# Earlier fetches of two sets, y stored in long rows, and gate loads in two halves, in the last stages of a gated decoder layer

## The chip, the cores and the metric

The kernel runs on one core of a Trainium2 chip. The metric is the device time of one execution in microseconds (us). The core's engines work side by side: TensorE (PE in the profile; PEld is its weight load) multiplies, VectorE (DVE), ScalarE (ACT) and GpSimd (POOL) work on elements, and SyncE (SP) issues transfers between DRAM and the core's memory. Each engine takes its instructions in order, so an instruction that waits holds up those behind it on the same engine.

## The reference

One decoder layer on 2048 rows of width 1024, in float32. From u = x * (1 + scale) + shift one wide product gives queries, keys, values, an attention gate, a pool input, a pool gate and two merge gates m_a and m_p. Then:

```
A = (sliding window attention * silu(attn_gate)) @ W_attn_proj
P = (causal pool, mixed and scaled, * silu(pool_gate)) @ W_pool_proj
y = (sigmoid(m_a) * A + sigmoid(m_p) * P) @ W_out * (1 + gate)
out = LayerNorm(alpha * x + y)
```

The last three lines and the two merge gates are what the change is about: the products with W_attn_proj, W_pool_proj and W_out behind the second attention.

## The kernel before, in words

The rows are worked on in two halves of 1024 (s = 0, 1). Each float32 product is made from split operands: a high part rounded to float32r and a low remainder, multiplied in three matmuls. A product of a 256 x 1024 piece of weights with a 1024 x 1024 operand goes by a scheme of seven block products in place of eight (B11, T1, T2, B21, T3, B22, T4), where the T's are sums and differences of blocks. The moving operand's seven blocks, each split, are the seven **sets** in SBUF; their raw blocks lie in DRAM in stores (`ain_d`, `pin_d`, `wo_d`), written by the attention and by `sums_to`. A pair of weight tiles is a **quad** (`Quad`, line 244 and on): `load` fetches it with three DMAs, `sum1`, `mid` and `late` make its sums on GpSimd, and `pair_split` (line 299 in the profile for the ScalarE part, 131 for the VectorE part) splits it for TensorE.

Behind the second attention the kernel runs six phases, in the loop at the end of the kernel function. Phase 0 finishes the last gate products. Phases 1 and 2 are the attention and pool projections for s = 0, phases 3 and 4 the same for s = 1; each has two groups of two quads. Phase 5 is the product with W_out, four groups of two quads; here y plays the part of the weights, and the rows y_d holds are loaded as quads (`out_quad`).

Within a phase `ring` goes through the groups. `back` does what a group has left after its fronts: for each quad T2 and B21, then T3 and B22, then T4, ten products of 12 matmuls. Then `front` does B11 and T1 for each quad of the next group, four products. After every product comes a `tick`; a group with a following one has ticks 0 to 13, 10 to 13 in the fronts. At a tick hooks run that are written for that place (a key (-1, p) is tick p of the phase's last group), and after them what `defer` has put off by that many ticks. So the order on SP is written out by hand, in program order (`sp` keeps each instruction behind the one traced before it on SP), while those written as `nc.scalar`, `nc.vector`, `nc.gpsimd` and `nc.sync` may be moved by the planner that orders each engine's list; a quad's weight loads are among these.

The next phase's sets replace the current ones during its last group. `FETCH_AT` says at which tick each set's raw halves (512 KB each) are fetched, `SPLIT_AT` at which tick ScalarE and VectorE split them: B11's halves at ticks 2 and 3, T1's at 4 and 5. The fetch writes the memory that TensorE reads as the set's low part, so it waits for the last product with the old set.

A quad of phases 1 to 4 has four finished blocks of 128 x 512 and multiplies each with a block of a merge gate, 256 KB, loaded by `ahead` into one of eight buffers. `back` begins with all eight loads of its two quads. In phases 1 and 3, and in the first group of 2 and 4, ScalarE takes the sigmoid of each loaded block. In the pool phases VectorE multiplies (line 601), GpSimd adds to the attention's part (line 603), and the sum is y, which is stored three ticks later. Beside all this `sums_to` makes the T blocks of coming stores: loads (`spare<-ain_B` and the like), subtractions on GpSimd, stores (`ain_T<-spare` and the like).

Of the kernel before, what the change touches and what calls it, by code (L numbers as in the profile page):

```python
# [19 lines left out]
P = 128  # L20
D = 1024
S = 2048
# [37 lines left out]
def kernel(  # L60
# [58 lines left out]
    ain_d = [set_store(f"ain{s}") for s in range(2)]  # L119
    pin_d = [set_store(f"pin{s}") for s in range(2)]  # L120
    gates_d = {n: dp.tile([2, KT, 2, P, CH], F32, name=f"{n}_d") for n in ("ag", "pg", "ma", "mp")}
    y_d = dp.tile([S // P, P, KT, P], F32, name="y_d")

    def cols(t, n):
        return t[:, n * CH : (n + 1) * CH]
# [118 lines left out]
    class Quad:  # L244
# [7 lines left out]
        def load(self, ph, own, q=nc.sync, e=nc.gpsimd):  # L252
            self.w, self.a22 = ph.weights(), ph.last(own)
            x = self.w
            q.dma_start(x[:, 2, :], self.srcs[1][:, 0:CH])
            q.dma_start(self.a22, self.srcs[1][:, CH:])
            q.dma_start(x[:, 0::3, :], by_two(self.srcs[0]))
            if e is not None:
                self.sum1(e)
# [75 lines left out]

    def back(ph, grp, opened, nxt, own, tick):
        st = []
        for turn in range(2):
            for q in grp:
                if q.ahead:  # L340
                    q.ahead(ph, turn)
        for q, (a, b, c, w, *copy) in zip(grp, opened):
            p5 = ph.p("p5")
            if w is None:
                c = bank("lg")
                nc.scalar.copy(c, a)
                nc.scalar.copy(p5, b)
                w = pair_split(ph, q.second())[::-1]
                q.late()
                product(c, w[1], "T2")  # L350
            else:
                u2 = copy[0] if copy else ph.p("u2")
                if not copy:
                    nc.scalar.copy(u2, a)
                if c is None:
                    c = bank("lg")
                    product(c, w[1], "T2", True)
                nc.vector.tensor_tensor(c, c, u2, ALU.add)
                nc.scalar.copy(p5, b)
            tick()  # L360
            nc.vector.tensor_tensor(b, c, p5, ALU.add)
            if not copy:
                product(a, w[0], "B21")
            tick()
            q.consume(ph, 0, 0, a)
            st.append((q, b, c, p5))
        w = {}

        def ask(q):

            defer(1, lambda: q.load(ph, own, nc.sync, None))
            defer(3, lambda: q.sum1(nc.gpsimd))

        def third(x):
            w[x] = pair_split(ph, st[x][0].third())[::-1]
            if x < len(nxt):
                ask(nxt[x])

        def with_t3(x):
            q, b, c, p5 = st[x]  # L380
            product(c, w[x][1], "T3")
            tick()
            nc.vector.tensor_tensor(p5, c, p5, ALU.add)
            q.consume(ph, 1, 1, p5)

        def with_b22(x):
            q, b, c, p5 = st[x]
            product(b, w[x][0], "B22")
            tick()
            q.consume(ph, 0, 1, b)  # L390

        for x in range(len(st)):
            third(x)
            with_t3(x)
            with_b22(x)
        for q in nxt[len(st) :]:
            ask(q)
        for q, b, c, p5 in st:
            w = half_split(ph, q.a22)
            product(c, w, "T4")  # L400
            tick()
            q.consume(ph, 1, 0, c)
# [29 lines left out]
    def defer(ticks, f):  # L432
        due.append((now[0] + ticks, len(due), f))
# [48 lines left out]

    SPLIT_AT = (2, 3, 4, 5, 6, 7, 11, 12, 13, 14, 15, 16, 17, 18)

    FETCH_AT = {"B11": 0, "T1": 0, "T2": 3, "B21": 4, "T3": 7, "B22": 8, "T4": 10}

    def set_steps(ph, store):

# [16 lines left out]
            todo.append((at, lambda n=name, h=half: split(n, h)))  # L505
        return sorted(todo, key=lambda t: t[0])

    def planned(hooks, ph, store, last, pending={}):
        if last:
            pending["steps"] = set_steps(ph, store)  # L510
        for p, f in pending["steps"]:
            if (p < 14) == last:
                hooks.setdefault((-1, p) if last else (0, p - 14), []).append(f)
        return hooks


# [79 lines left out]
    def pool_quad(s, m):  # L596
        gates, ahead = gates_ahead("mp", s, m, m < 4)

        def consume(ph, mi, t, src):
            g = gates.pop((mi, t))  # L600
            nc.vector.tensor_tensor(g, src, g, ALU.mult)
            dst = ta[m + mi][:, t * CH : (t + 1) * CH]
            nc.gpsimd.tensor_tensor(dst, g, dst, ALU.add)  # L603
            k = 8 * s + 4 * t
            to = y_d[k : k + 4, :, m + mi, :].rearrange("s p q -> p s q")
            defer(3, lambda: sp.dma_start(to, dst.rearrange("p (s q) -> p s q", s=4)))

        return Quad((wpp[m], wpp[m + 1]), consume, ahead)

# [41 lines left out]
    def last_norm(row, z):  # L651
# [6 lines left out]
        for n, q in enumerate((nc.sync, nc.scalar)):  # L658
            zn = cols(z, n)
            nc.vector.scalar_tensor_tensor(zn, zn, rs, cols(vec["lnb"], n), ALU.mult, ALU.add)  # L660
            q.dma_start(out[row * P : (row + 1) * P, n * CH : (n + 1) * CH], zn)

    def out_quad(k):
        def consume(ph, mi, n, src):
            row = k + mi
# [9 lines left out]
                else:  # L675
                    norm_row(ph, row, z)

        return Quad(tuple(y_d[k + i].rearrange("p k q -> p (k q)") for i in range(2)), consume)

# [773 lines left out]
    with Pools("mix", spare=4, p=2, c=8) as ph:  # L1455
# [15 lines left out]
        for i, (groups, store) in enumerate(phases):  # L1471
# [2 lines left out]
                planned(hooks, ph, store, False)  # L1474
            after, nxt = None, []
            if i + 1 < len(phases):
                planned(hooks, ph, phases[i + 1][1], True)
                nxt = phases[i + 1][0][0]
                after = lambda tick, nxt=nxt: [front(ph, q, tick) for q in nxt]
            else:  # L1480
# [67 lines left out]
```

## Time and profile before

| | |
|---|---|
| median of 3 runs | 1733.91 us (1731.9 to 1734.55) |
| profiled execution | 1734.67 us, span 1732.9 us |
| TensorE busy in the span | 1665.9 us (96%) |
| VectorE, ScalarE, GpSimd busy | 1257.8, 964.5, 1063.0 us |
| DMA engines, 1375 to 1455 us | 0.86 busy, 307 GB/s |
| phases 1 to 4 | about 1240 to 1577 us |

A row of the timeline gives the start in us, the time to the end of the row's instructions, engine, line, operation, what is written from what, sizes, how many instructions, and in brackets the idle time ahead of it and what ended it. L56 is the line of the helper that records most operations, so rows are told apart by their tiles: `w_set` is a split weight, `set_B` and `set_T` the B and T sets, `g` a gate block, `wide` the attention part and y, `W` and `A` a quad's raw weights. `lg` and `mm` are banks of TensorE's result memory: T2, T3 and T4 go to `lg`, the others to `mm`. A row that begins with SPq is SP's queue: the time of one is that of issuing it, with its wait for the ones in the row but not for the first.

### The profile page before, as it was taken

The page shows a single profiled execution, that of the slowest core. Times are in us where ns is not written, and L with a number is a line of the kernel's source. Part 1 is how long each engine was busy: PE and PEld are TensorE (multiplying, and loading weights), DVE is VectorE, ACT ScalarE, POOL GpSimd, SP SyncE. Part 2 cuts the span into 40 slices and gives each one's busy share as a digit, 9 for nine tenths or more (in the row PEclk, how much of TensorE's full clock was granted, in tenths as well). Part 3 has the DMA queues.
Part 4 walks back from the last instruction along what each step waited for, and adds up shares of the span by engine and source line. Part 5 has one row for each costly group of instructions (what it writes and reads, how often), then busy time and mean ns, then how long its engine had stood idle before and what let it go on. Part 6 is the DMA issues. An engine that isn't in the chain of part 4 may idle for free.

```text
span 1732.9 us, 24692 instructions
## 1 busy us (share of the span) xinstructions
PE 1665.9 (96%) x8056; PEld 1392.2 (80%) x8056; DVE 1257.8 (73%) x2256; ACT 964.5 (56%) x2002; POOL 1063.0 (61%) x782
## 2 busy tenths in 40 slices
PE   6899999999999999999999999999999899999997
PEld 5688888888888788887888888888777678777885
DVE  5966565787778768458578777786769487859777
ACT  4544446677677654334567676765644345434552
POOL 2054427686867837862476778594656796657442
PEclk9999999999999999999999999999999899999999
DMA  9378853323433377866533334235887788786432
GB/s 352 126 287 286 222 184 110 116 100 122 153 109 98 130 260 270 286 214 206 187 110 104 131 118 152 86 117 188 313 311 260 276 299 298 268 289 234 158 142 102
DMA packets 188721, 336.79 MB, mean 194 GB/s; under 512 B 18208, under 2 KB 43952, under 8 KB 188592
## 3 DMA queue, kind: packets, MB, share of 16 engines
q1 hardware_dynamic: 185472, 330.96, 55.4%
q10 hardware_dynamic: 3088, 4.23, 1.0%
q8 instruction: 64, 1.05, 0.3%
q14 instruction: 65, 0.53, 0.1%
q0 software_dynamic: 32, 0.02, 0.0%
HBM read 227.96 MB, written 110.33 MB: 195 GB/s over the span
## 4 chain that ended last, share of the span: by engine, by line
PE 44%; POOL 7%; DVE 6%; DMA 5%; issue 4%; ACT 2%; SPq 1%; POOLq 0%; DVEq 0%; ACTq 0%
PE mm L56 28%; PE lg L56 12%; PE pv L56 2%; POOL wide L603 2%; PE pt L56 2%; DVE w_set L131 2%; POOL spare L56 1%; POOL W L262 1%; SPq L56 1%; DVE set_T L56 1%; ACT w_set L299 1%; DMA W<-in_wap_dram 1%; DMA g<-ma_d 1%; POOL W L266 1%; POOL w_set L56 1%
## 5 line engine op out<-in xcount | busy, mean ns | idle before, releaser
L56 PE MATMUL mm<-set_B,w_set 128*128 128x512 f32 x2664 | 660.1, 395 | 9.9 <-ACT w_set L299 5.2
L56 PEld LDWEIGHTS mm<-set_B,w_set 128*128 128x128 f32 x2664 | 499.1, 190 | 119.1 <-DVE w_set L131 8.4
L56 PE MATMUL mm<-set_T,w_set 128*128 128x512 f32 x1824 | 457.5, 397 | 4.5 <-POOL w_set L56 1.2
L56 PE MATMUL lg<-set_T,w_set 128*128 128x512 f32 x1728 | 424.7, 396 | 20.3 <-DVE w_set L131 8.6
L56 PEld LDWEIGHTS lg<-set_T,w_set 128*128 128x128 f32 x1728 | 326.9, 191 | 96.6 <-DVE w_set L131 14.6
L56 PEld LDWEIGHTS mm<-set_T,w_set 128*128 128x128 f32 x1824 | 337.2, 189 | 77.0 <-DVE mm L56 4.4
L131 DVE TENSOR_TENSOR w_set<-W,w_set 128x1024 fp32r<-128x1024 f32 x138 | 207.9, 1507 | 173.9 <-ACT w_set L299 164.0
L299 ACT CAST w_set<-W 128x1024 fp32r<-128x1024 f32 x138 | 144.9, 1050 | 283.1 <-PE mm L56 165.6
L56 POOL TENSOR_TENSOR w_set<-W,w_set 128x512 fp32r<-128x512 f32 x132 | 171.9, 1310 | 101.2 <-ACT w_set L56 91.3
L262 POOL TENSOR_TENSOR W<-W,A 128x512 f32<-128x512 f32 x46 | 71.5, 1554 | 218.1 <-DMA A<-in_win_dram 75.5
L56 ACT ACTIVATE L<-L,nm 128x257 f32<-128x257 f32 (+1 forms) x256 | 127.1, 498 | 26.4 <-DVE nm L56 20.3
L56 POOL TENSOR_TENSOR W<-W 128x512 f32<-128x512 f32 x82 | 108.3, 1334 | 51.6 <-DVE sm L56 30.3
L271 POOL TENSOR_TENSOR W<-W 128x512 f32<-128x512 f32 x46 | 74.7, 1624 | 98.5 <-DVE w_set L131 89.0
L56 POOL TENSOR_TENSOR spare<-spare 128x512 f32<-128x512 f32 x68 | 121.0, 1782 | 13.0 <-DMA spare<-ain_B 9.1
L56 DVE CUSTOM_DVE_ANT_0 L<-lg,bt,nsink 128x256 f32<-128x256 f32 (+1 forms) x256 | 111.6, 473 | 20.4 <-DMA bt<-e_rep 9.4
L56 ACT CAST w_set<-W 128x512 fp32r<-128x512 f32 (+1 forms) x164 | 100.1, 626 | 38.2 <-POOL W L56 25.7
L56 DVE COPY o<-pv 64x256 f32<-64x256 f32 x128 | 54.3, 424 | 81.1 <-PE pv L56 79.8
L56 ACT CAST pth<-pt 128x512 fp32r<-128x512 f32 (+1 forms) x128 | 72.8, 568 | 63.3 <-PE pt L56 62.9
L56 ACT ACTIVATE L<-L,sm 128x256 f32<-128x256 f32 (+1 forms) x128 | 64.3, 503 | 68.1 <-DVE sm L56 67.8
L266 POOL TENSOR_TENSOR W<-W 128x512 f32<-128x512 f32 x44 | 75.0, 1705 | 34.2 <-DVE w_set L131 25.1
L267 POOL TENSOR_TENSOR W<-W 128x512 f32<-128x512 f32 x44 | 74.4, 1691 | 31.6 <-DMA W<-in_win_dram 26.0
L56 DVE TENSOR_SCALAR L<-L,sm 128x256 f32<-128x256 f32 (+1 forms) x128 | 89.9, 702 | 0.0
(225 smaller groups left out, 2468.3 us busy)
## 6 DMA issues: line engine op xcount, KB each, us to landing
W<-in_win_dram SPq DMA_DIRECT2D x42, 512.0 KB, 5.5
W<-in_win_dram SPq DMA_DIRECT2D x42, 256.0 KB, 3.7
A<-in_win_dram SPq DMA_DIRECT2D x42, 256.0 KB, 4.6
ag_d<-sig SPq DMA_DIRECT2D x32, 256.0 KB, 5.1
pg_d<-sig SPq DMA_DIRECT2D x32, 256.0 KB, 4.6
pg<-pg_d SPq DMA_DIRECT2D x32, 256.0 KB, 3.1
pin_B<-fin SPq DMA_DIRECT2D x32, 256.0 KB, 2.1
ag<-ag_d SPq DMA_DIRECT2D x32, 256.0 KB, 2.8
```

Source lines behind the costliest of these rows:

```text
L56: return lambda *args, **kw: self.tc.keep_in_program_order(op(*args, **kw))
L131: engine.tensor_tensor(dst, src, as32(hi), ALU.subtract)
L262: e.tensor_tensor(self.w[:, 1, :], self.w[:, 2, :], self.a22, ALU.add)
L266: e.tensor_tensor(x[:, 1, :], x[:, 1, :], x[:, 0, :], ALU.subtract)
L267: e.tensor_tensor(x[:, 2, :], x[:, 0, :], x[:, 2, :], ALU.subtract)
L271: e.tensor_tensor(x[:, 3, :], x[:, 3, :], x[:, 1, :], ALU.subtract)
L299: a.copy(by_two(hi), raw)
L603: nc.gpsimd.tensor_tensor(dst, g, dst, ALU.add)
```

## The change

Three things, all in the phases behind the second attention.

- The fetches of B11 and T1 for the next phase move from tick 0 of a phase's last group to ticks 12 and 13 of the group ahead of it. Where a phase has one group (phase 0), they stay at tick 0 of the last group.
- `back` begins with the four first gate loads of its two quads, and puts the other four off by two ticks.
- y lies in DRAM by blocks, as the gates do, so a block of 128 x 512 is stored in rows of 2 KB and not in four pieces of 512 bytes. A quad of phase 5 is then read in pieces of 512 bytes, with four DMAs of 256 KB in place of three.

```
-    y_d = dp.tile([S // P, P, KT, P], F32, name="y_d")
+    y_d = dp.tile([2, KT, 2, P, CH], F32, name="y_d")
...
         def load(self, ph, own, q=nc.sync, e=nc.gpsimd):
             self.w, self.a22 = ph.weights(), ph.last(own)
             x = self.w
+            if len(self.srcs[0].shape) == 3:
+                for dst, src, half in ((x[:, 2, :], 1, 0), (self.a22, 1, 1), (x[:, 0, :], 0, 0), (x[:, 3, :], 0, 1)):
+                    q.dma_start(dst.rearrange("p (k q) -> p k q", k=4), self.srcs[src][:, 4 * half : 4 * half + 4, :])
+                if e is not None:
+                    self.sum1(e)
+                return
...
     def back(ph, grp, opened, nxt, own, tick):
         st = []
-        for turn in range(2):
-            for q in grp:
-                if q.ahead:
-                    q.ahead(ph, turn)
+        for q in grp:
+            if q.ahead:
+                q.ahead(ph, 0)
+                defer(2, lambda q=q: q.ahead(ph, 1))
...
-    FETCH_AT = {"B11": 0, "T1": 0, "T2": 3, "B21": 4, "T3": 7, "B22": 8, "T4": 10}
+    FETCH_AT = {"B11": -2, "T1": -1, "T2": 3, "B21": 4, "T3": 7, "B22": 8, "T4": 10}
...
-    def planned(hooks, ph, store, last, pending={}):
+    def planned(hooks, ph, store, last, pending={}, groups=()):
         if last:
             pending["steps"] = set_steps(ph, store)
         for p, f in pending["steps"]:
             if (p < 14) == last:
-                hooks.setdefault((-1, p) if last else (0, p - 14), []).append(f)
+                at = (-1, p) if last else (0, p - 14)
+                if p < 0:
+                    at = (-2, 14 + p) if len(groups) > 1 else (-1, 0)
+                hooks.setdefault(at, []).append(f)
         return hooks
...
             nc.gpsimd.tensor_tensor(dst, g, dst, ALU.add)
-            k = 8 * s + 4 * t
-            to = y_d[k : k + 4, :, m + mi, :].rearrange("s p q -> p s q")
-            defer(3, lambda: sp.dma_start(to, dst.rearrange("p (s q) -> p s q", s=4)))
+            defer(3, lambda: sp.dma_start(y_d[s, m + mi, t], dst))
...
+    def y_row(row):
+        return y_d[row // 8, :, row // 4 % 2, :, row % 4 * P : (row % 4 + 1) * P].rearrange("k p q -> p k q")
...
-        return Quad(tuple(y_d[k + i].rearrange("p k q -> p (k q)") for i in range(2)), consume)
+        return Quad(tuple(y_row(k + i) for i in range(2)), consume)
...
-                planned(hooks, ph, phases[i + 1][1], True)
+                planned(hooks, ph, phases[i + 1][1], True, groups=groups)
```

## The prediction

> **What bounds the kernel.** I read the page first, then TensorE's rows in order of time behind the second attention (from about 1226 us), the waits, the DMA queue's rows of SP, and windows of 4 us.
>
> ```profile
> PE 1665.9 (96%) x8056; PEld 1392.2 (80%) x8056; DVE 1257.8 (73%) x2256; ACT 964.5 (56%) x2002; POOL 1063.0 (61%) x782
> ```
>
> TensorE is the bound, so the change can only win back what TensorE loses. In these stages every product is 12 matmuls, and the rows below stand 2.72 us apart where nothing waits. A group of two quads is 14 products: 38.08 us. These rows are the first product of each group (T2 of its first quad), from phase 1 to phase 5:
>
> ```profile
> 1277.99 2.88 PE L56 MATMUL lg<-set_T,w_set 128*128 128x512 f32 x12
> 1321.49 3.09 PE L56 MATMUL lg<-set_T,w_set 128*128 128x512 f32 x12
> 1359.78 2.98 PE L56 MATMUL lg<-set_T,w_set 128*128 128x512 f32 x12
> 1416.59 2.88 PE L56 MATMUL lg<-set_T,w_set 128*128 128x512 f32 x12
> 1454.78 2.88 PE L56 MATMUL lg<-set_T,w_set 128*128 128x512 f32 x12
> 1494.16 3.02 PE L56 MATMUL lg<-set_T,w_set 128*128 128x512 f32 x12
> 1532.38 2.88 PE L56 MATMUL lg<-set_T,w_set 128*128 128x512 f32 x12
> 1576.97 0.61 PE L56 MATMUL lg<-set_T,w_set 128*128 128x512 f32 x2
> ```
>
> The second groups of phases 1 to 4, which I call places 1 to 4, take 43.50, 56.81, 39.38 and 44.59 us: they lose 5.42, 18.73, 1.30 and 6.51 us, 31.96 in all. The first groups between them lose 0.1 to 0.2 each. So this is the most that the change can find here, and places 2 and 4 hold most of it. What ends the loss at these two, on TensorE and on ScalarE:
>
> ```profile
> 1378.50 1.22 PE L56 MATMUL lg<-set_T,w_set 128*128 128x512 f32 x2 [5.68 <-ACT w_set L299]
> 1388.50 2.89 PE L56 MATMUL lg<-set_T,w_set 128*128 128x512 f32 x12
> 1408.06 5.90 PE L56 MATMUL mm<-set_B,w_set 128*128 128x512 f32 x12 [3.08 <-ACT w_set L299]
> ```
>
> ```profile
> 1375.11 1.04 ACT L56 CAST set_B<-set_B 128x1024 fp32r<-128x1024 f32 x1 [8.39 <-DMA set_B<-ain_B]
> 1541.43 1.05 ACT L56 CAST set_B<-set_B 128x1024 fp32r<-128x1024 f32 x1 [7.49 <-DMA set_B<-wo_B]
> ```
>
> ScalarE, in order, stands 8.39 us at the split of the next phase's B11 because its data has not landed; the weight split that TensorE's T3 needs is queued behind it, and TensorE stands 5.68 us. The two matmuls behind it take 1.22 us, where the two at 1576.97 take 0.61. Place 4 has the same wait, 7.49 us.
>
> Why the data is late, on SP:
>
> ```profile
> 1271.54 5.78 SPq L56 DMA_DIRECT2D g<-ma_d  x8
> 1277.63 1.21 SPq L56 DMA_DIRECT2D set_B<-pin_B  x2
> 1359.07 5.22 SPq L56 DMA_DIRECT2D y_d<-wide  x2
> 1364.35 3.84 SPq L56 DMA_DIRECT2D g<-mp_d  x8
> 1368.76 1.23 SPq L56 DMA_DIRECT2D set_B<-ain_B  x2
> 1448.15 3.76 SPq L56 DMA_DIRECT2D g<-ma_d  x8
> 1452.00 1.28 SPq L56 DMA_DIRECT2D set_B<-pin_B  x2
> 1529.70 3.87 SPq L56 DMA_DIRECT2D g<-mp_d  x8
> 1533.66 1.44 SPq L56 DMA_DIRECT2D set_B<-wo_B  x2
> ```
>
> ```profile
> 1360.00:1364.00 4.00, 4.00 (x19) 3.16 (x18) 0.13 (x1) 0.00 (x0) 3.92 (x4) 1.00 0.21 64
> 1372.00:1376.00 4.00, 0.82 (x4) 0.36 (x2) 0.00 (x0) 0.89 (x1) 0.00 (x0) 1.00 1.05 407
> 1392.00:1396.00 4.00, 4.00 (x20) 3.30 (x19) 3.96 (x4) 0.71 (x1) 4.00 (x3) 1.00 1.06 405
> ```
>
> In each place eight gate loads go out ahead of the B11 fetch, and at place 2 SP first stood behind two y stores. The windows (busy PE, PEld, DVE, ACT, POOL, then clock, DMA share, GB/s) show the DMA engines at 0.21 just before and full from 1372 on: the fetch is asked for at the start of a jam.
>
> **The change, part by part.**
>
> *B11 and T1 asked for earlier.* They move from tick 0 of the last group to ticks 12 and 13 of the group ahead, past the eight gate loads. Each gets a wait in exchange: the set is being read by TensorE until the last B11 (T1) front ends. That is the start of the next product (first rows below; the second rows are issues from 1200 us on: how many, KB each, median us from issue to landing):
>
> ```profile
> 1275.27 2.88 PE L56 MATMUL mm<-set_T,w_set 128*128 128x512 f32 x12
> 1357.06 2.88 PE L56 MATMUL mm<-set_T,w_set 128*128 128x512 f32 x12
> 1452.06 2.88 PE L56 MATMUL mm<-set_T,w_set 128*128 128x512 f32 x12
> 1529.66 2.88 PE L56 MATMUL mm<-set_T,w_set 128*128 128x512 f32 x12
> ```
>
> ```profile
> set_B<-ain_B SPq DMA_DIRECT2D x10, 512.0 KB, 8.1
> g<-ma_d SPq DMA_DIRECT2D x32, 256.0 KB, 5.3
> y_d<-wide SPq DMA_DIRECT2D x32, 256.0 KB, 3.2
> A<-y_d SPq DMA_DIRECT2D x8, 256.0 KB, 3.4
> ```
>
> Place 2: B11's set is free at 1357.06, but SP reaches the fetch behind the first of the two y stores of 1359.07 (the second, of the last T4, comes after tick 12's hooks): 1359.5, 9.2 us earlier, into idle DMA. Even with the median 8.1 us it lands at 1367.6; ScalarE gets there at 1366.7 (1375.11 less 8.39). I take the whole 8.39 as gone and the following work on VectorE and POOL as that much earlier: gain 8.4. Not the 10.4 that T3 to T3 loses beyond the earlier stall (1388.50 less six products from 1359.78 is 12.4, of which some 2 precede it): POOL is busy 4.00 of 4 us from 1388 on, and the second stall, at 1408.06, waits for it. That stall is what is late next, and I keep it. Ends: 4.4 (the fetch behind both y stores, 1364.4) and 16.8 (all 18.73 but the first 2).
>
> Place 4: the set is free at 1529.66, SP issues at about 1529.8 instead of 1533.66: 3.9 us of the 7.49 go. Ends 0 and 6.5.
>
> Place 1: 1275.4 instead of 1277.63, and its T3 stalls come from a crowded ScalarE and VectorE, not from the fetch. I take 1 us of 5.42; ends -7.8 (below) and 5.4.
>
> Place 3: the set is free at 1452.06 and the fetch goes out at 1452.00 today: nothing to gain; 0, ends -7.9 and 1.3.
>
> In phase 0, with one group, the fetch stays where it is: 0.
>
> *Behind the new waits.* SP stands until TensorE is done; behind it are the last y store, stores of the sums, and the gate loads. T1's fetch goes out at the start of the group, its two issues take some 1.3 us, and then come the gates: 1279.3 instead of 1271.54 at place 1, 1365.7 instead of 1364.35, 1456.1 instead of 1448.15, 1533.7 instead of 1529.70: 7.8, 1.3, 7.9 and 4.0 later. Who waits: in the attention phases ScalarE's sigmoid, and VectorE's multiplication of the first finished bank. Place 3 shows the room:
>
> ```profile
> 1460.74 0.68 DVE L592 TENSOR_TENSOR wide<-mm,g 128x512 f32<-128x512 f32 x1
> 1461.34 1.72 DVE L131 TENSOR_TENSOR w_set<-W,w_set 128x1024 fp32r<-128x1024 f32 x1
> ```
>
> A gate asked for at 1456.1 lands by 1461.4 (5.3), and with 0.6 for the sigmoid the multiplication starts at 1462.0, 1.3 late; the weight split behind it ends at 1463.1 and T3 needs it at 1465.7 (1454.78 and four products). 2.6 us of room cover 1.3: I cost this at 0. Without that cover it is up to 7.9.
>
> That SP itself stands for TensorE is in its own waits (total us, times, longest):
>
> ```profile
> SPq L56 <- PE lg L56: 23.4, 14, 5.6
> ```
>
> The Trainium skill, "DMA: Bandwidth & Descriptors", section "Anatomy of one DMA", has the rule that speaks against this change: a semaphore wait stands at the issuing sequencer and not in the DMA engines, so whatever is queued behind the fetch is held with it; the row agrees. If nothing made room for that, the time would be the third rival's.
>
> *Gates in two halves.* Same sixteen loads a phase, four of them two ticks later, past tick 0's and tick 1's stores of sums. The late half serves B22 and T4, three products (8.2 us) or more behind its issue against a landing of 5.3: 0; end -3, where those stores wait long for POOL and the sigmoids of a first group stand ahead of T3's split.
>
> *y in rows of 2 KB.* 32 stores become long rows; the loads of the out stage become 512-byte rows, four issues a quad instead of three. A store with 512-byte rows lands after 3.2 us, a load with 2 KB rows after 3.4: the row length does not show. Eight more issues of about 0.4 us on SP lie beside products; a quad's load in the out stage has this much room:
>
> ```profile
> 1590.76 1.29 POOL L262 TENSOR_TENSOR W<-W,A 128x512 f32<-128x512 f32 x1 [5.56 <-DMA W<-y_d]
> 1605.38 2.88 PE L56 MATMUL mm<-set_B,w_set 128*128 128x512 f32 x12
> ```
>
> The sum is ready at 1592 and its front begins at 1605: a load twice as slow is still hidden. 0; ends -1.6 and 1.6, the 0.2 us between the two landings on each of eight quads.
>
> **Sum.** 8.4 + 3.9 + 1 + 0 = 13.3 us. The profiled execution took 1734.67 us (span 1732.9 and 1.8 around it), which gives 1721.4; the median of the three runs is 0.8 below it, so 1721 against 1733.91.
>
> **Rivals.**
>
> *Everything behind goes too.* If POOL, which now idles while VectorE stands, uses that time and the second stall at place 2 goes, and the tail of place 4: 16.8 + 6.5 + 5.4 = 28.7, or 1705. For it: POOL has no work in 1372 to 1376. Against: 4.00 of 4 later.
>
> *The fetch is not much earlier.* If at places 2 and 4 it gets out only behind the last y store: 4.4 and 2.5 (1531.1, when that store is out) instead of 8.4 and 3.9, less 1 for the sums: 6 us, 1728. For it: y stores hold SP 5.22 us here. Against: only one of them stands ahead of tick 12's hooks.
>
> *Slower: the gates are held.* The new wait on SP delays them by 7.8 + 1.3 + 7.9 + 4.0 = 21.0 us. If ScalarE's sigmoids or VectorE's multiplications stand ahead of the weight split of T2 or T3, this reaches TensorE. It decides from 13.3 of the 21.0 on; with 17 it is +3.7, 1738. For it: at place 1 ScalarE already stands for a gate, 3.47 us (row below). Against: the room at place 3; and this order of ScalarE is not fixed by the source.
>
> ```profile
> 1277.59 1.31 ACT L581 ACTIVATE g<-g 128x512 f32<-128x512 f32 x2 [3.47 <-DMA g<-ma_d]
> ```
>
> **How the numbers follow.** Forecast 0.55 (1714 to 1730), everything 0.14, not much earlier 0.12, gates held 0.19. A measurement of this kernel tells about 0.2% (3.5 us) from no change. Faster than that: 0.53 + 0.14 + 0.07 = 0.74; same: 0.02 + 0.05 + 0.02 = 0.09; slower 0.17. The range leaves out the lower half of the second case (0.07) and the upper half of the last (0.10): 1707 to 1736.
>
> **What would show it.** SP's rows should have the B11 fetch ahead of the gates at all four places, at place 2 by about 9 us; ScalarE's wait for set_B from ain_B should be gone and the one for wo_B about half; place 2 should take some 48 us, place 4 some 41, places 1 and 3 as before; in the out stage no product should wait for a load of y. Wrong would be: ScalarE or VectorE standing for g at places 1 or 3 with TensorE behind, or place 2's second stall grown by what the first gave up.

## The result and the profile after

The changed kernel takes 1728.22 us, the median of 12 runs (1726.14 to 1732.47), against 1734.23 for the kernel before on the same chip: a ratio of 0.9967, with a 95% interval from 0.9959 to 0.9975. That is 6.0 us faster, where 12.9 were forecast. The sign was right and the time lies inside the range, but the gain is under half of the forecast.

The profiled execution took 1731.03 us (span 1729.2), 3.6 us less than the one of before and 2.8 more than its own median. The two traces can therefore account for some 3.6 us; the rest of the 6.0 is known from the medians only. From the page of the changed kernel, the busy times:

```profile
PE 1664.1 (96%) x8056; PEld 1392.5 (81%) x8056; DVE 1254.5 (73%) x2256; ACT 964.2 (56%) x2002; POOL 1058.1 (61%) x782
```

The first product of each group on TensorE, as in the prediction (start, length, engine, line, operation, tiles):

```profile
1277.18 2.88 PE L56 MATMUL lg<-set_T,w_set 128*128 128x512 f32 x12
1317.18 3.07 PE L56 MATMUL lg<-set_T,w_set 128*128 128x512 f32 x12
1355.75 0.61 PE L56 MATMUL lg<-set_T,w_set 128*128 128x512 f32 x2
1410.07 2.88 PE L56 MATMUL lg<-set_T,w_set 128*128 128x512 f32 x12
1450.02 2.88 PE L56 MATMUL lg<-set_T,w_set 128*128 128x512 f32 x12
1492.36 2.88 PE L56 MATMUL lg<-set_T,w_set 128*128 128x512 f32 x12
1530.44 2.88 PE L56 MATMUL lg<-set_T,w_set 128*128 128x512 f32 x12
1572.79 0.61 PE L56 MATMUL lg<-set_T,w_set 128*128 128x512 f32 x2
```

Differences of neighbouring rows give the groups. Places 1 to 4 now take 40.00, 54.32, 42.34 and 42.35 us, where they took 43.50, 56.81, 39.38 and 44.59. So place 1 won 3.5, place 2 won 2.5, place 4 won 2.2, and place 3 lost 3.0. The first group of phase 3, which lost 0.1 before, takes 39.95 instead of 38.19: 1.8 lost. From the start of place 1 to phase 5 this is 295.61 us against 298.98, 3.4 less.

SP's rows show the fetches where they were expected. A row has start, time, queue, line, kind, tiles and how many issues it holds:

```profile
1273.07 1.89 SPq L56 DMA_DIRECT2D set_B<-pin_B  x2
1277.71 2.40 SPq L56 DMA_DIRECT2D g<-ma_d  x4
1356.89 1.19 SPq L56 DMA_DIRECT2D set_B<-ain_B  x2
1362.05 2.20 SPq L56 DMA_DIRECT2D g<-mp_d  x4
1445.90 1.89 SPq L56 DMA_DIRECT2D set_B<-pin_B  x2
1450.56 2.51 SPq L56 DMA_DIRECT2D g<-ma_d  x4
1526.33 1.89 SPq L56 DMA_DIRECT2D set_B<-wo_B  x2
1530.97 7.44 SPq L56 DMA_DIRECT2D g<-mp_d  x8
```

Counted from its group's start, the fetch goes out at +1.14 at place 2, where it was +8.98: 7.8 us earlier. At place 4 it is -4.11 instead of +1.28. The price is in the rows of g: at place 4 the gates, which went out at -2.68, now go out at +0.53, and their eight issues take 7.44 us.

What became of place 2, on TensorE, ScalarE and GpSimd of the changed kernel (in brackets the idle time ahead of a row and what ended it; L305 and L268 are the lines that the prediction's rows have as L299 and L262):

```profile
1370.85 2.56 PE L56 MATMUL lg<-set_T,w_set 128*128 128x512 f32 x10 [1.13 <-DVE w_set L131]
1392.66 5.34 PE L56 MATMUL mm<-set_B,w_set 128*128 128x512 f32 x12 [5.39 <-ACT w_set L305]
1403.34 4.07 PE L56 MATMUL mm<-set_B,w_set 128*128 128x512 f32 x10 [0.53 <-DVE w_set L131]
```

```profile
1363.04 1.99 ACT L56 CAST set_B<-set_B 128x1024 fp32r<-128x1024 f32 x2
1391.56 1.04 ACT L305 CAST w_set<-W 128x1024 fp32r<-128x1024 f32 x1 [9.52 <-DMA pin_T<-spare]
```

```profile
1389.06 1.25 POOL L612 TENSOR_TENSOR wide<-g,wide 128x512 f32<-128x512 f32 x1
1390.27 1.25 POOL L268 TENSOR_TENSOR W<-W,A 128x512 f32<-128x512 f32 x1
```

The same sum and the same front in the kernel before:

```profile
1393.53 1.73 POOL L262 TENSOR_TENSOR W<-W,A 128x512 f32<-128x512 f32 x1
1399.38 2.88 PE L56 MATMUL mm<-set_B,w_set 128*128 128x512 f32 x12
```

ScalarE splits B11 at 1363.04 without a wait: the 8.39 us are gone, and with them the stall of 5.68 at T3 (1.13 is left). But at the first front of phase 3, where TensorE did not wait before, it now stands for 5.39 us, and the twelve matmuls behind it take 5.34 where 2.88 is usual. The stall that the prediction kept, 3.08 us at the second front with twelve matmuls in 5.90 behind it, shrank to 1.37 and 0.53 us.

At the first front TensorE waits for ScalarE's split of a weight. That split starts 0.04 us behind the end of GpSimd's sum (line 268, `sum1`; 1390.27 and 1.25), so I take it to wait for the sum, although its row names a store. The sum stands in GpSimd's list behind additions into y (line 612). Counted from the group's start, TensorE is ready for this front at +31.5 us instead of +39.6, 8.1 earlier and so nearly the 8.4 forecast. The sum starts at +34.5 instead of +33.8: it did not come earlier at all. What the first stall gave up, the new one took.

### The profile page after: what moved, and what is told of

Read it like the earlier page. It is cut to its first block, busy times and chain, and to the rows that moved or that the text cites. A ratio compares the mean times of both kernels' runs of the same rounds, so it can differ in the third digit from the quotient of the medians.

```text
span 1729.2 us, 24722 instructions
## 1 busy us (share of the span) xinstructions
PE 1664.1 (96%) x8056; PEld 1392.5 (81%) x8056; DVE 1254.5 (73%) x2256; ACT 964.2 (56%) x2002; POOL 1058.1 (61%) x782
## 4 chain that ended last, share of the span: by engine, by line
PE 47%; POOL 7%; DVE 5%; DMA 4%; issue 4%; ACT 1%; SPq 0%; POOLq 0%; DVEq 0%; ACTq 0%
PE mm L56 30%; PE lg L56 13%; PE pv L56 2%; PE pt L56 2%; DVE w_set L131 1%; POOL spare L56 1%; POOL nxt L56 1%; POOL W L268 1%; POOL w_set L56 1%; POOL fin L56 1%; DMA W<-in_wpp_dram 1%; DMA W<-in_wap_dram 1%; DMA pin_T<-spare 1%; POOL wide L612 1%; DVE set_T L56 1%
## 5 line engine op out<-in xcount | busy, mean ns | idle before, releaser
L56 PE MATMUL lg<-set_T,w_set 128*128 128x512 f32 x1728 | 417.9, 392 | 10.0 <-DVE w_set L131 4.8
L131 DVE TENSOR_TENSOR w_set<-W,w_set 128x1024 fp32r<-128x1024 f32 x138 | 198.4, 1439 | 185.9 <-ACT w_set L305 172.8
L305 ACT CAST w_set<-W 128x1024 fp32r<-128x1024 f32 x138 | 144.8, 1050 | 291.0 <-PE mm L56 164.4
L268 POOL TENSOR_TENSOR W<-W,A 128x512 f32<-128x512 f32 x46 | 70.6, 1535 | 223.8 <-DVE set_T L56 58.2
L56 POOL TENSOR_TENSOR spare<-spare 128x512 f32<-128x512 f32 x68 | 117.2, 1725 | 12.6 <-DMA spare<-ain_B 8.7
```

What stands on the lines that cost most here:

```text
L56: return lambda *args, **kw: self.tc.keep_in_program_order(op(*args, **kw))
L131: engine.tensor_tensor(dst, src, as32(hi), ALU.subtract)
L268: e.tensor_tensor(self.w[:, 1, :], self.w[:, 2, :], self.a22, ALU.add)
L305: a.copy(by_two(hi), raw)
```

## The experiments

All kernels are timed against the kernel before. The times of the places come from each kernel's own profiled execution, by the same rows; y alone, which is no difference in time, moves place 1 by 2.0 us and place 3 by 3.3, so a difference of that size at one place counts only where rows show what made it. The last column is place 2 with the first group of phase 3, for a reason that comes out below. The last three kernels have the pinned sums too.

| kernel | ratio (95%) | place 1 | place 2 | place 3 | place 4 | place 2 + next group |
|---|---|---|---|---|---|---|
| before | 1 | 43.50 | 56.81 | 39.38 | 44.59 | 95.00 |
| changed | 0.9967 (0.9959 to 0.9975) | 40.00 | 54.32 | 42.34 | 42.35 | 94.27 |
| fetch alone | 0.9972 (0.9961 to 0.9982) | 42.89 | 50.97 | 39.95 | 42.25 | 91.02 |
| y alone | 1.0007 (0.9997 to 1.0016) | 41.47 | 56.32 | 42.69 | 42.97 | 94.51 |
| halves alone | 0.9957 (0.9943 to 0.9971) | 40.53 | 56.30 | 39.41 | 39.72 | 94.38 |
| changed, sums pinned | 0.9977 (0.9966 to 0.9988) | 40.67 | 49.99 | 41.97 | 42.51 | 90.00 |
| halves and fetch | 0.9964 (0.9952 to 0.9977) | 42.21 | 51.47 | 40.30 | 41.45 | 91.54 |
| changed, T1 late | 0.9968 (0.9957 to 0.9980) | 40.48 | 53.47 | 40.32 | 40.82 | 93.38 |
| halves, fetch at place 2 | 0.9949 (0.9934 to 0.9964) | 40.57 | 53.21 | 39.45 | 39.69 | 93.12 |
| the same, sums pinned | 0.9947 (0.9930 to 0.9963) | 40.38 | 50.89 | 39.43 | 39.65 | 91.08 |
| halves by one tick | 1.0034 (1.0022 to 1.0046) | 40.13 | 54.35 | 38.44 | 38.62 | 102.48 |
| pinned, B21 late | 0.9964 (0.9951 to 0.9977) | 40.97 | 52.00 | 43.15 | 38.58 | 91.91 |
| gates first, fetch everywhere | 0.9925 (0.9913 to 0.9938) | 38.59 | 50.73 | 39.48 | 38.61 | 90.52 |
| gates first, fetch at place 2 | 0.9912 (0.9899 to 0.9926) | 38.59 | 51.06 | 39.43 | 38.62 | 89.31 |
| gates first, no early fetch | 0.9916 (0.9902 to 0.9930) | 38.68 | 52.94 | 40.05 | 38.63 | 91.13 |
| gates first, second sum early | 0.9919 (0.9907 to 0.9931) | 38.59 | 44.38 | 39.48 | 38.63 | 89.92 |

### The three parts, each alone

The first kernel has only the new FETCH_AT and what `planned` does with it; the second only y in long rows; the third only this in `back`:

```
-        for turn in range(2):
-            for q in grp:
-                if q.ahead:
-                    q.ahead(ph, turn)
+        for q in grp:
+            if q.ahead:
+                q.ahead(ph, 0)
+                defer(2, lambda q=q: q.ahead(ph, 1))
```

> The change's first part alone: B11 and T1 asked for in the fronts of the group ahead; gates whole, y as before. First theory (the fetch makes both the gain and the new stall): 4 to 8 us faster than the kernel before, like the whole change; at place 2 ScalarE no longer waits for set_B and the second stall (the two fronts behind the last T4) is longer than before by most of what the first gave up. Second theory (the rows of y bring the gain): no more than 2 us faster. Third theory (the split gates cost something that hides part of the gain): 9 to 13 us faster.

> The rows of y alone: stores of 2 KB rows, loads of 512-byte rows; fetches and gates as before. First theory: within 2 us of the kernel before. Second theory: 4 us or more faster, as stores land sooner and SP gets on. If loads in short rows cost: 2 us or more slower, with products of the out stage waiting.

> The gate loads in two halves alone; fetches at tick 0 as before. First theory: the fetch stands behind the four first gate loads and two ticks' work instead of eight loads, so it goes out some 2 us earlier; 0 to 3 us faster. Third theory: 2 to 5 us slower, with VectorE or ScalarE waiting for a gate of the second half.

Measured: 1730.31, 1735.2 and 1727.22 us against 1735.1. y in long rows is no difference (its interval holds 1). The fetch alone gives 4.9 us. The surprise is the halves: costed at 0 by the prediction and expected at 0 to 3 us, they give 7.5 us, as much as the whole change (the intervals overlap). Their rows at place 4, on SP and ScalarE:

```profile
1524.15 1.97 SPq L56 DMA_DIRECT2D g<-mp_d  x4
1526.22 1.19 SPq L56 DMA_DIRECT2D set_B<-wo_B  x2
1529.02 2.16 SPq L56 DMA_DIRECT2D g<-mp_d  x4
```

```profile
1531.76 1.05 ACT L56 CAST set_B<-set_B 128x1024 fp32r<-128x1024 f32 x1 [2.63 <-DMA set_B<-wo_B]
```

The group starts at 1527.57. With four gate loads ahead of it in place of eight, the fetch of tick 0 goes out at -1.35 instead of +1.28, and ScalarE's wait for it falls from 7.49 to 2.63 us. The first half of the gates is not later than before (-3.42 against -2.68). So at place 4 the halves alone are an earlier fetch, and one that holds no gate of the first half.

Place 2 shows the other side. There SP still stands behind the two y stores, the fetch goes out at +8.16 instead of +8.98, and the place takes 56.30 us, as before. At place 1 more than the fetch moves: eight sigmoids stood on ScalarE ahead of the split of B11, which then waited 0.70 us for its data, and with the halves four do.

### GpSimd's order at place 2

In the changed kernel the planner put six of place 2's additions ahead of the sum for phase 3's first front, where the kernel before has four. This kernel keeps the additions and the sums in program order:

```
-            defer(3, lambda: q.sum1(nc.gpsimd))
+            defer(3, lambda: q.sum1(pool))
...
-            nc.gpsimd.tensor_tensor(dst, g, dst, ALU.add)
+            pool.tensor_tensor(dst, g, dst, ALU.add)
```

> The whole change, and on POOL the sums of the next weights and the adds into y are kept in program order, so the sum for the first front of phase 3 stands ahead of the last adds of place 2 again. If the place of that sum in POOL's list makes the new stall: place 2 some 5 us shorter than with the change, 1723 to 1725 us. If the weights themselves land too late (the DMA engines are full there), the sum waits for them at its new place: place 2 within 2 us of the change, 1727 to 1730 us.

Measured: 1731.13 us, 0.9977. Place 2 takes 49.99 us, but the group ahead of it 41.01 instead of 38.57, and the time, expected at 1723 to 1725, is not better than the changed kernel's. The order matters at the place, and what it won there the time does not show.

### Do the parts add up, and are the gates held?

> The changed kernel with y stored as before: the earlier fetch and the gates in two halves together. If the two parts give what each gave alone, 4.9 us for the fetch and 7.5 for the halves, it takes 1722. My theory is that they do not add up, because both move the same fetch of B11 ahead of gate loads, and the early one holds the gates: it then takes 1726 to 1730, with place 4 at 42 us as in the changed kernel and not at 39.7 as with the halves alone. Place 3 settles the long rows of y: if they cost there, it is back at 39.5 to 40 us; if its 42 us are another matter, it stays.

> The changed kernel with T1 fetched at tick 0 as before, behind the first four gate loads; only B11 is early. Theory: at place 4 the gates are held by the wait of T1's fetch for the last T1 front, and this reaches TensorE through the multiplications, GpSimd's additions and the sums of the next weights. Then the gates go out some 2 to 4 us earlier, the first addition at place 4 comes less than 8 us behind the group's start instead of 9.1, and the place takes 39.5 to 40.5 instead of 42.35; the time is 1725 to 1727. If the gates have nothing to do with it, place 4 stays at 42 and the time within 1 us of the changed kernel. If GpSimd is moved into another order there, this run cannot tell, and the lists are to be compared.

> Gates in two halves, y as before, and the early fetch only where phase 2 hands over to phase 3 (place 2). Theory: places 1, 3 and 4 stand as with the halves alone (40.5, 39.4, 39.7 us), and place 2 falls from 56.3 by the first stall, but part comes back at its second stall because the planner puts two additions ahead of the sum for phase 3's first front: 51 to 54. Time 1722 to 1725. The rival, that the early fetch costs in places that follow it, would give no more than the halves alone, 1727.

> The run above, with GpSimd's order at place 2 pinned to program order for the additions into y of that group and the two sums for phase 3's first fronts; ScalarE's and VectorE's lists are the same in both. Theory: the sum stands two additions (some 3 us) earlier, the second stall at place 2 shrinks by as much, place 2 takes 49 to 51 us, time 1719 to 1722. The rival is that the stall waits for the weights, which land late from a full set of DMA engines: then the order changes nothing, place 2 stays within 1 us of the run above, and so does the time.

The first is the changed kernel with y as before. The others:

```
-    FETCH_AT = {"B11": -2, "T1": -1, ...
+    FETCH_AT = {"B11": -2, "T1": 0, ...
...
-                    at = (-2, 14 + p) if len(groups) > 1 else (-1, 0)
+                    at = (-2, 14 + p) if store is ain_d[1] else (-1, 0)
...
+            defer(3, lambda: q.sum1(pool if getattr(q, "pin", False) else nc.gpsimd))
+        quad.pin = s == 1 and m < 4
+            (pool if s == 0 and m >= 4 else nc.gpsimd).tensor_tensor(dst, g, dst, ALU.add)
```

Measured against 1735.6: halves and fetch 1729.52, T1 late 1730.06, fetch at place 2 only 1726.19, and this with pinned sums 1727.27. So the two parts do not add up: 4.9 and 7.5 us alone, 6.2 together (by the ratios). Leaving the early fetch out at places 1, 3 and 4 made those places 4.2 us shorter (42.21, 40.30, 41.45 against 40.57, 39.45, 39.69) and the median 3.3 less (the intervals overlap, 0.9952 to 0.9977 and 0.9934 to 0.9964): so there the fetch seems to cost rather than to bring.

T1 late was a miss: place 4 came out at 40.82, between the two expectations, and the time did not move. Its rows say why. The gates are held no longer: VectorE's first multiplication at place 4 starts at +5.6 us, where it started at +8.4 in the changed kernel, and the first addition into y comes at +6.4. But T1, fetched later, makes VectorE wait 0.92 and 0.74 us for T1's splits a little further on.

The pinned sums are a half hit. With ScalarE's and VectorE's lists the same, place 2 fell from 53.21 to 50.89, so the order was worth 2.3 us there, but the time, expected at 1719 to 1722, did not follow. In the profile of the pinned run GpSimd stands 1.61 us ahead of the sum. The row names nothing that ended it; the weights, asked for from 1381.74 on, land 7.2 to 8.4 us after their issue there, so I take it to wait for them:

```profile
1390.19 2.35 POOL L56 TENSOR_TENSOR W<-W,A 128x512 f32<-128x512 f32 x1 [1.61 <-issue]
```

### Later set loads, halves by one tick, gates first

Three questions: whether full DMA engines hold those weights, whether the halves work by the fetch's place, and what it is worth when no gate is held at all. For the last, the first four gates of a second group are asked for at the start of the fronts ahead of it, in front of the early fetch.

```
+            todo.append((FETCH_AT[name] + 2 * (name == "B21" and store is ain_d[1]), ...
...
+                defer(1, lambda q=q: q.ahead(ph, 1))
...
             if gi + 1 < len(groups):
+                for q in groups[gi + 1]:
+                    if q.ahead:
+                        q.ahead(ph, 0)
+                        q.asked = True
                 opened = [front(ph, q, tick) for q in groups[gi + 1]]
```

> The halves alone, with the second four gate loads put off by one tick and not two: they still go out behind the fetch of tick 0, but right behind it. Theory: the halves gain because the fetch of B11 stands behind four gate loads and not eight; then this gains the same, 7.5 us, places 1 and 4 at 40.5 and 39.7, time 1727 to 1729. The rival, that it helps that the second gates and their sigmoids come later, would give at most half of it, 1731 or more. GpSimd's list comes out in another order than with two ticks, so a time in between would tell little; the fetch's rows in the trace then decide.

> The pinned run for place 2, with phase 3's B21 fetched two ticks later there, so that the two quads' weights for phase 3's first fronts are asked for ahead of 1 MB of set loads. Theory: what is left of the second stall at place 2 is the weights' landing from a full set of DMA engines (asked for at 1381.7, GpSimd's sum starts at 1390.2); with the first of them asked for some 1.3 us earlier and 1 MB less ahead of it, it lands 2 to 3 us earlier, and place 2 goes from 50.9 to 48 or 49, the time down by 2 us. If GpSimd's own work is the limit, place 2 stays at 50.5 to 51.5.

> The changed kernel with y as before, and the first four gate loads of every second group asked for at the start of the fronts ahead of it, before the early fetch. So the fetch is early at all four places and holds no gate of the first half. Theory: at place 4 the cost of the held gates goes (the first addition comes less than 8 us behind the group's start, the place takes 39 to 40 and not 41.5), place 1 takes 40 or less and not 42.2, and the time is 1722 to 1726 against 1729.5 with the gates behind the fetch. If the early fetch costs there for another reason, the bandwidth that it takes from stores and sums, the places stay at 41 to 42 and the time at 1728 to 1730.

> The pinned run with the early fetch at place 2 alone, and the first four gate loads ahead of the group as in the run above. If the gates matter at all places, this is the fastest: places 1 to 4 at 39.5, 49 to 50, 39.4 and 39, time 1719 to 1724. If gates at tick 0 without an early fetch in front are early enough, it takes the pinned run's 1727.

Measured against 1733.78: 1739.89, 1728.87, 1721.77 and 1719.26.

The halves by one tick are slower than before, which no theory had. At places 1 and 4 they do what the halves do (40.13 and 38.62). At place 4, whose gates take no sigmoid, the fetch goes out at -3.03 and ScalarE's wait for it is 0.71 us: its place explains the gain. At place 1 this run does not tell the fetch's place from the sigmoids, of which four stand ahead of the split here too. The loss is in the first groups of phases 1 and 3, 45.09 and 48.13 us, which move no fetch. There the planner put six sigmoids (five in phase 3) ahead of a set's split on ScalarE, and TensorE stood for the split; these are the rows in phase 1, and phase 3 has two waits of the same kind, 2.24 and 3.75 us:

```profile
1253.16 3.23 ACT L581 ACTIVATE g<-g 128x512 f32<-128x512 f32 x6
1256.30 1.03 ACT L56 CAST set_B<-set_B 128x1024 fp32r<-128x1024 f32 x1
```

```profile
1257.38 0.50 PE L56 MATMUL mm<-set_B,w_set 128*128 128x512 f32 x1 [2.32 <-ACT set_B L56]
1259.38 5.06 PE L56 MATMUL mm<-set_B,w_set 128*128 128x512 f32 x11 [1.50 <-DVE set_B L56]
```

B21 late was a miss. The first of the two sums did come 1.3 us earlier in its group and without a wait (+27.6 instead of +28.9), but then TensorE stood 2.08 us at the first front and 4.10 at the second, and place 2 took 52.00. So an earlier landing brought that sum forward, and the place gained nothing. Place 3 took 43.15.

Gates first did what was expected and a little more: with the fetch early at all four places and no gate of the first half held, 1721.77 us (1722 to 1726 expected), the time that was forecast for the change. Places 1 and 4 come within 0.6 us of the ideal 38.08. Rows of that run at place 4 (its group starts at 1523.24):

```profile
1513.86 1.95 SPq L56 DMA_DIRECT2D g<-mp_d  x4
1519.13 1.89 SPq L56 DMA_DIRECT2D set_B<-wo_B  x2
1523.82 2.46 SPq L56 DMA_DIRECT2D g<-mp_d  x4
```

VectorE and TensorE of this run, the first multiplication with a gate, the split of the weights for the next phase's first front, and that front:

```profile
1528.88 0.69 DVE L615 TENSOR_TENSOR g<-mm,g 128x512 f32<-128x512 f32 x1 [0.24 <-PE mm L56]
1549.21 1.71 DVE L131 TENSOR_TENSOR w_set<-W,w_set 128x1024 fp32r<-128x1024 f32 x1
1550.44 3.10 PE L56 MATMUL mm<-set_B,w_set 128*128 128x512 f32 x12
```

The same in the changed kernel, whose group starts at 1530.44, and the first multiplication of halves and fetch, whose group starts at 1527.97:

```profile
1538.81 0.69 DVE L610 TENSOR_TENSOR g<-mm,g 128x512 f32<-128x512 f32 x1 [2.98 <-PE lg L56]
1558.90 1.69 DVE L131 TENSOR_TENSOR w_set<-W,w_set 128x1024 fp32r<-128x1024 f32 x1
1560.64 4.14 PE L56 MATMUL mm<-set_B,w_set 128*128 128x512 f32 x10 [2.02 <-DVE w_set L131]
```

```profile
1535.50 0.69 DVE L610 TENSOR_TENSOR g<-mm,g 128x512 f32<-128x512 f32 x1 [2.12 <-DMA g<-mp_d]
```

The multiplication starts at +5.6 us with the gates first, at +7.5 in halves and fetch, where its row names the gate, and at +8.4 in the changed kernel. There the row names a product of TensorE that ended at the same moment; the gates landed 5.4 to 7.9 us (median 7.7) after their issues from 1530.97 on, so I take it to wait for the gate as well. From this multiplication on VectorE has no idle time in the profile until the split is done at 1560.59, and TensorE, which stood 2.02 us for it, starts then. That is how a held gate reaches TensorE at the first front: through VectorE's own list, some 22 us later. GpSimd's sum of those weights comes later too, at 23.4 us behind the group's start instead of 19.2, in part because four additions into y stand ahead of it and not three. But ScalarE's half of the split, which waits for that sum, is done at 1556.67, so the sum is not what ends this stall.

A second pair has the same edit where the fetch is early at place 2 alone: "the same, sums pinned" and "gates first, fetch at place 2" in the table. It gave 6.1 us there (0.9947 to 0.9912), although no early fetch held the gates of places 1, 3 and 4. So most of the 6.8 us that it gave to halves and fetch (0.9964 to 0.9925) need not be the hold: the gates simply go out earlier than in the kernel before, and no longer stand ahead of the fetch.

### Is it the fetch at all, and what is left at place 2?

Two kernels from the fastest one: without any early fetch (FETCH_AT as before), and with the sum for phase 3's second front two ticks earlier on GpSimd, which leaves the lists of ScalarE, VectorE and SP the same.

```
+            pin = getattr(q, "pin", False)
+            defer(1 if pin and q is nxt[1] else 3, lambda: q.sum1(pool if pin else nc.gpsimd))
```

> The run before it (first four gates ahead of the group, two halves, pinned sums) without any early fetch: B11 and T1 at tick 0 at all four places. Theory: the early fetch has its own worth at place 2 only, where SP otherwise stands behind y stores and the DMA engines fill: place 2 goes back from 51.1 to 53 or more (the first stall at T3 returns), the time from 1719.3 to 1722 to 1725. If the gates' place was all that mattered, place 2 stays within 1 us and the time within 2 us of 1719.3: then the early fetch is worth nothing by itself.

> The fastest run so far, with GpSimd's sum for phase 3's second front written two ticks earlier; ScalarE's, VectorE's and SP's lists are the same word for word, and on GpSimd only that sum and the two operations of the first front's weights stand ahead of two additions and a subtraction. Theory: what is left of the second stall at place 2 is GpSimd's order, the sum at 1395.5 having waited behind work of 12 us though its data was asked for at 1378 to 1379.5: it then ends at about 1391 instead of 1396.7, the stall of 4.09 us at 1397.9 goes with the slow clock behind it, place 2 takes 44 to 47 us and the time 1713 to 1716. If the weights' landing from full DMA engines is the limit, the sum waits for its data, place 2 stays at 50 to 51.5 and the time at 1718 to 1721.

Measured against 1733.76: 1718.28 and 1719.4. Without the early fetch, expected at 1722 to 1725 if the fetch has a worth of its own, no difference can be told: 0.9916 (0.9902 to 0.9930) against 0.9912 (0.9899 to 0.9926). Its place 2 is 1.9 us longer in the profile, as expected in kind, and as 0.0011 of the time that would be hidden in these intervals. The fetch is not late in this kernel either: with no gate ahead of it, that of tick 0 goes out at -3.37 us at place 4, where it was +1.28 in the kernel before, and at +6.25 instead of +8.98 at place 2.

The earlier sum did at place 2 what was expected, 44.38 us instead of 51.06, and gave all of it back in the next group, which took 45.54 instead of 38.25; the time, expected at 1713 to 1716, did not move. First the kernel it was made from, then the one with the sum early, GpSimd and TensorE:

```profile
1395.49 1.26 POOL L56 TENSOR_TENSOR W<-W,A 128x512 f32<-128x512 f32 x1
...
1397.88 5.86 PE L56 MATMUL mm<-set_B,w_set 128*128 128x512 f32 x12 [4.09 <-ACT w_set L305]
```

```profile
1390.46 2.27 POOL L56 TENSOR_TENSOR W<-W,A 128x512 f32<-128x512 f32 x1
1406.36 1.28 POOL L273 TENSOR_TENSOR W<-W 128x512 f32<-128x512 f32 x1
1407.60 1.26 POOL L272 TENSOR_TENSOR W<-W 128x512 f32<-128x512 f32 x1
1412.50 8.99 POOL L56 TENSOR_TENSOR spare<-spare 128x512 f32<-128x512 f32 x4
...
1395.13 2.60 PE L56 MATMUL mm<-set_B,w_set 128*128 128x512 f32 x10 [0.20 <-DVE w_set L131]
1409.98 5.89 PE L56 MATMUL lg<-set_T,w_set 128*128 128x512 f32 x12 [2.87 <-ACT w_set L305]
```

The stall of 4.09 us is gone. The additions that the sum passed now stand ahead of the next weights' operations (lines 273 and 272), and TensorE stands 2.87 us at T2 behind those, again with slow matmuls after it. Windows over place 2 and the group behind it, one for each of the two kernels (busy PE, PEld, DVE, ACT, POOL, then clock, DMA share, GB/s):

```profile
1355.30:1444.60 89.30, 81.35 (x338) 63.97 (x336) 67.07 (x55) 39.17 (x52) 76.49 (x43) 0.96 0.89 309
```

```profile
1355.90:1445.80 89.90, 81.92 (x337) 63.97 (x336) 67.32 (x55) 39.04 (x52) 75.24 (x43) 0.96 0.89 307
```

GpSimd is busy for 75 to 76 us in the stretch of 89 to 90 in both orders, and the stretch keeps its length. So this order moved the loss along it and did not take it away. That GpSimd's amount of work, and not the DMA engines at 0.89, sets the 13 to 14 us still lost there (76.16 would be ideal) is what these rows suggest; no run took work off GpSimd or bytes off the DMA engines alone, so this stays open.

## Why the prediction came out as it did

**Place 2, forecast 8.4 us.** The mechanism of the first stall was right in each link: SP earlier by 7.8 us (9.2 forecast), no wait at ScalarE, the T3 stall down from 5.68 to 1.13. The step that failed is "the following work on VectorE and POOL as that much earlier", and with it "That stall is what is late next, and I keep it". TensorE came to the first front 8.1 us earlier in its group, GpSimd's sum for that front 0.8 later, behind two additions more. So a stall of 5.39 us stands where none was, with twelve matmuls in 5.34 behind it; the kept stall at the second front fell from 3.08 to 1.9. The place won 2.5, and the group behind it, which the sum did not price at all, lost 1.8. Place 2 and the next group together went from 95.00 to 94.27. The prediction's last paragraph names an outcome of this kind, place 2's second stall grown, as one that would make it wrong, but the sum gave it no price; the row of GpSimd busy 4.00 of 4 us was read as a reason not to expect more, when it was a reason to expect less. The runs put some 2.3 us of the place down to the planner's order of GpSimd (the pinned pair), and in the last pair another order moved the loss into the next group.

**Place 4, forecast 3.9.** ScalarE's wait went, and the place won 2.2. The step that failed is "I cost this at 0", for the gates behind the new waits. Room was looked for at place 3, for one multiplication ahead of one weight split, with 5.3 us for a gate's landing. At place 4 the gates took 7.7 us (median), the multiplication stood 2.98 us, and VectorE, with no idle time from there on, split the weights of the next phase's first front so late that TensorE stood 2.02 us and the ten matmuls behind it took 4.14 us in place of 2.56. With the halves alone place 4 takes 39.72; with halves and early fetch 41.45 to 42.35. The early fetch seems to cost 4.2 us at places 1, 3 and 4 in the profiles and 3.3 by the medians, whose intervals overlap. Putting the gates ahead of it gave 6.8 us (0.9964 to 0.9925), but the gates also go out earlier than before there, and this alone can bring most of it. So the hold is seen in the rows of place 4, and its price in the time stays open. The rival "gates held" named this path in part; its 17 of 21 us did not come.

**Place 1, forecast 1, and place 3, forecast 0.** Place 1 won 3.5, place 3 lost 3.0. Neither is settled by single executions: the kernel with only y changed, which does nothing new at place 1, stood there for 41.47. At place 3 the 42 to 43 us come in kernels with y in long rows (changed, y alone, pinned) but not in all of these (40.32 with T1 late), and once with y as before (43.15). In the first two of these and in the last, TensorE's wait for ScalarE at the second front is 1.44 to 1.91 us and the ten matmuls behind it take 3.81 to 4.15; with T1 late it is 1.03 and they take 2.58. Why the weight's sum comes later in some kernels stays open.

**Gates in two halves, forecast 0, end -3.** Wrong, and outside its ends: alone they give 7.5 us. The prediction counted what the late half could lose and not what stands behind the eight loads on SP. The fetch of tick 0 was the next thing in that queue, by the very rows quoted to explain why its data was late.

**y in long rows, forecast 0.** Right: 1.0007 (0.9997 to 1.0016).

**The other rivals.** "The fetch is not much earlier" gave 1728, which is the time that came, but not for its reason: the fetch went out 7.8 us earlier at place 2 and 5.4 at place 4. "Everything behind goes too" did not happen in any kernel at place 2, the run with 44.38 us included, since the group behind it paid.

**The sum.** The parts were added as if they were independent. Two of them move the same fetch past the same gate loads, so the second brings little once the first is there: 4.9 and 7.5 us alone, 6.2 together. The forecast's 1721 was reached, by 1721.77, only when the gates were put ahead of the fetch; and then the early fetch itself could be left out with no loss that these runs can tell, 1718.28. What was ascribed to the new places in `FETCH_AT` came as well from the order of gates and fetch on SP, which sends the fetch out earlier too.

## What to carry to other kernels

When something is moved forward in an in-order queue, cost the entry that it passes as carefully as the one that gains, and follow it to the end of the other engines' lists: a held load reached TensorE here through VectorE's list, some 22 us later. When a stall is taken away ahead of an engine that is busy all through the next stretch, price the next stall as growing, and judge an edit by the sum of the stretch and not by the place. Parts that act on the same wait must be tried apart, since one that was costed at nothing may hold as much as the whole.

## What the runs showed of the hardware that was not expected

GpSimd's operation on 128 x 512 has two prices. Windows of the kernel with the second sum early:

```profile
1404.00:1408.00 4.00, 3.12 (x14) 2.25 (x12) 0.00 (x1) 0.00 (x0) 4.00 (x4) 1.00 1.10 364
1412.00:1416.00 4.00, 4.00 (x11) 3.12 (x10) 4.00 (x4) 2.73 (x4) 3.92 (x3) 0.50 0.72 276
```

Where VectorE is idle (0.00 of 4 us), GpSimd's rows above stand 1.24 us apart; where VectorE is busy all the time (4.00), four operations take 8.99 us, 2.25 each. So VectorE's work in this stretch makes GpSimd's longer, which the prediction's costs did not have. The Trainium skill, "SBUF — State Buffer", section "Who interferes with whom", says that a VectorE operation on two operands in SBUF contends with GpSimd's reads for a port pair that one holds at a time; the rows agree with that.

A stall of TensorE can cost more than its length: behind waits of 2.87, 4.09 and 5.39 us, twelve matmuls took 5.89, 5.86 and 5.34 us in place of 2.88, and the granted clock behind the first was 0.50 over 4 us (the second row above). The Trainium skill, "TensorE: Matmul & The Clock Gate", section "Part 1: The HAM clock gate (the "warmup" mystery)", puts the fall to half rate behind an idle window of about 3.4 us; here 2.87 us were enough. Shorter stalls did either: behind 2.02 us in the changed kernel ten matmuls took 4.14 us, behind 2.08 us in the run with B21 late 2.55.
